# Transposing attention probabilities in row halves, and one written TensorE order for the dilated attention stage

## The chip, the cores and the metric

The kernel runs on one core of a Trainium2 chip. The metric is the device time of one execution in microseconds (us). Five queues of instructions matter here: TensorE (PE in the rows; its weight loads are shown apart as PEld), VectorE (DVE), ScalarE (ACT), GpSimd (POOL, idle here) and SyncE (SP), which issues the DMAs. Each runs its own list in order and waits on semaphores of the others.

## The reference, cut to what matters

The kernel is a two-layer encoder trunk over 256 tokens of width 1024. Layer 0 mixes tokens with a dilated attention (mixer A), layer 1 with a windowed grouped-query attention (mixer B). Each layer is FFN, mixer, FFN, gated embedding; the four FFNs are most of the work.

```python
for i in range(DEPTH):                                    # DEPTH = 2
    h = h + 0.5 * rms_norm(swiglu(rms_norm(h, g[0]), ffn_wi[i, 0], ffn_wo[i, 0]), g[1])
    hn = rms_norm(h, g[2])
    y = dilated_mixer(hn, ...) if i == 0 else window_gqa_mixer(hn, ...)
    h = h + rms_norm(y, g[3])
    h = h + 0.5 * rms_norm(swiglu(rms_norm(h, g[4]), ffn_wi[i, 1], ffn_wo[i, 1]), g[5])
    ...
# inside a mixer, per head: s = q @ k.T * dh**-0.5, masked; pr = exp(s - max); den = sum(pr)
#                           o = (pr @ v) / den;  then all heads: o @ wo
# mixer A: 3 dilation groups x 8 heads, outputs mixed by their denominators (one softmax over
#          the 512 allowed keys of the three groups); mixer B: 16 query heads on 4 key heads
```

## The kernel before, in words

The 256 tokens are two tiles of 128 (t = 0, 1). Weights are split into two float32r parts, so a projection of one tile against 512 columns is 24 multiplies (`proj`, L193; `rowprods`, L204). ScalarE makes the high part (L87) and VectorE the low part (L90) of every weight, all through the kernel.

**Mixer A** (`mixer_a`) runs nine projection blocks of 2 x 24 multiplies: values, queries and keys of three dilation groups. `block` leaves the transposition of queries and keys (`heads_T`, L316) pending, and the middle of the next block issues it. Then come eight *units*, each one token tile and one pair of heads: tile 0 with pairs 0 to 3, then tile 1. A unit n has these steps, which the rest of this document calls by letters:

- **S(n)**, `scores`: the logits of two heads (L325), 64 rows of the array for each head, one head on rows 0 to 63 and one on rows 64 to 127, into two PSUM banks "y" (four exist).
- the softmax (`soft`), for each of the two heads: on VectorE mask and maximum (L396), on ScalarE exponential with its sum (L397), on VectorE reciprocal (L398) and scaling (L399).
- **T(n)**, `transpose_p`: the scaled probabilities, four blocks of 128 x 128 for each head, by TensorE against the identity (L336) into one PSUM bank "t" for each head (two exist), copied to SBUF by ScalarE (L338).
- **PV(n)**, `values`: times the values (L414), one head on array columns 0 to 63, one on 64 to 127, into a bank "a"; ScalarE and VectorE split the result (L72, L73).

After four units `finish` multiplies tile 0 by the output weights (24 multiplies, L204) and `boundary` normalises and adds; the same for tile 1 at the end. `attend` emits these steps with S two units ahead of PV, but TensorE's list is set by the scheduler of the tile framework: only what stands inside one `tc.manual_schedule` (S of one unit, PV of one unit) keeps its written order there, and the scheduler weaves the pieces of several units into each other. The last projection block holds S(0) in its middle.

**Mixer B** has the same steps: its lines are L531 for S, L543, L546, L548 and L550 for the softmax (two halves of 256 keys for each head), the same `transpose_p` and L568 for PV, the same `attend`, and 48 multiplies for each output projection.

A multiply with plain float32 operands (all PV, all scores of mixer A) stands twice in the trace, once for each of its two passes; a transposition stands once.

Of the kernel before, what the change touches and what calls it, by code (L numbers as in the profile page):

```python
# [8 lines left out]
F32 = mybir.dt.float32  # L9
# [5 lines left out]
P = 128  # L15
# [4 lines left out]
DH = 64  # L20
# [17 lines left out]
def trunk_kernel(ctx, tc, x, p, norm_g, ffn_wi, ffn_wo, ple_proj, ple_gate, a_wqkv, a_wo,  # L38
                 b_wqkv, b_wo, b_sink, rope, mask_a, mask_b, out):
    nc = tc.nc  # L40
# [4 lines left out]
    wts = pool("wts", 9)  # L45
    hgs = pool("hgs", 1)
    m4 = pool("m4", M4)
    w2 = pool("w2", 12)
    ps_y = pool("ps_y", 4, space=bass.MemoryType.PSUM)
    ps_a = pool("ps_a", 2, space=bass.MemoryType.PSUM)  # L50
    ps_t = pool("ps_t", 2, space=bass.MemoryType.PSUM)
# [9 lines left out]
    def w2_tile(shape, dt=F32):  # L61
        return w2.tile(shape, dt, name="w2t", tag="w2t")
# [4 lines left out]
    def bank(which, shape=(P, 512)):  # L67
        pl = {"y": ps_y, "a": ps_a, "t": ps_t}[which]
        return pl.tile(list(shape), F32, name=f"ps{which}", tag=f"ps{which}")
# [260 lines left out]
    def pv_out(o_ps, oT, slot):  # L330
        split(oT[:, 0, slot, :], oT[:, 1, slot, :], o_ps[:, 0:P])

    def transpose_p(sm_of, kts):
        pt = bank("t")
        for i, a in enumerate(kts):
            nc.tensor.transpose(pt[:, i * P:(i + 1) * P], sm_of(a), ident)  # L336
        pT = w2_tile([P, 4, P])
        nc.scalar.copy(pT, pt.rearrange("p (n q) -> p n q", n=4))  # L338
        return pT

    def out_proj(t, oTs, ws, y):
# [2 lines left out]
    def mixer_a(acts, gb, row):  # L344
# [18 lines left out]
        def block(kind, g):  # L363
            ws = [weight_kt2(a_wqkv[0], c, ((kind * 3 + g) * 512,)) for c in range(4)]
            if kind == 2:
                dst = V[g] = m4_tile([P, 2, 512])
            else:
                dst = (qT, kT)[kind][g] = ([m4_tile([P, 4, 256], F32R) for _ in range(2)] if g == 0 and SPLIT_A
                                           else [m4_tile([P, 4, 256])])

            def one(t, mid=flush):
                ps = bank("a")
                proj(ps, acts[t], ws, mid)
                if kind == 2:
                    nc.scalar.activation(dst[:, t, :], ps, AF.Copy, scale=acts[t].rstd)  # L375
                    return
                q = w2_tile([P, 512])
                nc.scalar.activation(q, ps, AF.Copy, scale=nscale(t) if kind == 0 else acts[t].rstd)
                rope_(q, t, 8)
                pend.append(lambda: heads_T(q, dst, t, 4))  # L380
            return one
# [20 lines left out]
        oT, pTs = {}, {}  # L402

        def trans(t, pr):
            pTs[t, pr] = [transpose_p(lambda i: sm[:, i * P:(i + 1) * P], range(4)) for sm in sms.pop((t, pr))]

        def values(t, pr):
            pT = pTs.pop((t, pr))
            o_ps = bank("a")
            with tc.manual_schedule(engines={E.PE}):  # L410
                for i, (g, kt) in enumerate(((0, 0), (0, 1), (1, t), (2, t))):
                    for u in range(2):
                        hd = 2 * pr + u
                        nc.tensor.matmul(o_ps[64 * u:64 * u + 64, 0:P], V[g][:, kt, hd * DH:(hd + 1) * DH],  # L414
                                         pT[u][:, i, :], start=(i == 0), stop=(i == 3))
            if pr == 0:
                oT[t] = m4_tile([P, 2, 4, P], F32R)
            pv_out(o_ps, oT[t], pr)

        b0 = block(2, 0)  # L420
        b0(0)
        b1 = block(2, 1)
        b1(0, acts[1].fin)
        b0(1)
        b1(1)
        for g in range(3):
            for kind in range(2):
                b = block(kind, g)
                b(0)
                b(1)  # L430
        b = block(2, 2)
        b(0)
        sms = {}
        units = [(t, pr) for t in range(2) for pr in range(4)]

        def score(n):
            if n < len(units):
                sms[units[n]] = scores(*units[n])

        b(1, lambda: score(0))  # L440
        return attend(units, score, trans, values, 1,
                      [lambda k=k: weight_rows(a_wo[0], k) for k in range(4)],
                      lambda t: [oT[t]], gb, row)

    def attend(units, score, trans, values, done, wload, oTs, gb, row, flush=nothing):
        ahead = AHEAD
# [25 lines left out]
    def mixer_b(acts, gb, row):  # L472
# [80 lines left out]
        oT, pTs = {}, {}  # L553

        def trans(t, pr):
            pTs[t, pr] = [transpose_p(lambda n: sm[:, n // 2, (n % 2) * P:(n % 2 + 1) * P], range(4))
                          for sm in sms.pop((t, pr))]

        def values(t, pr):
            a, ih = pr // 2, pr % 2  # L560
            pT = pTs.pop((t, pr))
            o_ps = bank("a")
            with tc.manual_schedule(engines={E.PE}):
                for i in range(2):
                    for kt in range(2):
                        for u in range(2):
                            kv = 2 * a + u
                            nc.tensor.matmul(o_ps[64 * u:64 * u + 64, i * P:(i + 1) * P],  # L568
                                             V[:, kt, kv * DH:(kv + 1) * DH], pT[u][:, 2 * i + kt, :],
                                             start=(kt == 0), stop=(kt == 1))  # L570
            if ih == 0:
                oT[t, a] = m4_tile([P, 2, 4, P], F32R)
            o = oT[t, a]
            split(o[:, 0, 2 * ih:2 * ih + 2, :].rearrange("p n q -> p (n q)"),
                  o[:, 1, 2 * ih:2 * ih + 2, :].rearrange("p n q -> p (n q)"), o_ps[:, 0:256])
# [196 lines left out]
```

## Time and profile before

| | us |
|---|---|
| median of 3 runs (1093.93 to 1094.2) | 1093.97 |
| the profiled execution | 1094.63 |
| its span, first to last instruction | 1092.9 |
| TensorE busy | 1066.1 (98%) |
| VectorE busy | 694.8 (64%) |
| ScalarE busy | 570.6 (52%) |

Times in rows are microseconds from the start of the span. A matmul's busy time contains its latency in the pipeline, so that in a run of them the step from one start to the next start tells what they cost, and a TensorE that is 100% busy need not be at its peak. "PEclk" is the granted clock, 1.00 for 2.4 GHz and 0.50 for 1.2 GHz. What an engine waited for stands behind a row as [idle before <- releaser].

### The profile page before, as it was taken

The page shows a single profiled execution, that of the slowest core. Times are in us where ns is not written, and L with a number is a line of the kernel's source. Part 1 is how long each engine was busy: PE and PEld are TensorE (multiplying, and loading weights), DVE is VectorE, ACT ScalarE, POOL GpSimd, SP SyncE. Part 2 cuts the span into 40 slices and gives each one's busy share as a digit, 9 for nine tenths or more (in the row PEclk, how much of TensorE's full clock was granted, in tenths as well). Part 3 has the DMA queues.
Part 4 walks back from the last instruction along what each step waited for, and adds up shares of the span by engine and source line. Part 5 has one row for each costly group of instructions (what it writes and reads, how often), then busy time and mean ns, then how long its engine had stood idle before and what let it go on. Part 6 is the DMA issues. An engine that isn't in the chain of part 4 may idle for free.

```text
span 1092.9 us, 14763 instructions
## 1 busy us (share of the span) xinstructions
PE 1066.1 (98%) x5110; PEld 862.5 (79%) x5110; DVE 694.8 (64%) x1523; ACT 570.6 (52%) x896; POOL 0.7 (0%) x6
## 2 busy tenths in 40 slices
PE   7999999999999999999999999999998999999996
PEld 6888888788877888888887888887866888888885
DVE  6765454865666855576588654655975875557465
ACT  5644343655565645454456444544675665446343
POOL 0000000000000000000000000000000000000000
PEclk8999999999999999999999999999999999999998
DMA  8865655565540575576544756655660565567601
GB/s 268 294 199 176 204 182 165 174 221 164 174 135 30 165 229 187 161 246 205 163 138 154 233 170 195 193 162 167 178 170 1 158 214 180 171 211 241 202 1 39
DMA packets 130235, 189.04 MB, mean 173 GB/s; under 512 B 9440, under 2 KB 100320, under 8 KB 130160
## 3 DMA queue, kind: packets, MB, share of 16 engines
q1 hardware_dynamic: 130160, 188.10, 54.8%
q8 instruction: 40, 0.66, 0.2%
q14 instruction: 35, 0.29, 0.1%
HBM read 187.02 MB, written 1.05 MB: 172 GB/s over the span
## 4 chain that ended last, share of the span: by engine, by line
PE 93%; DVE 3%; ACT 2%; DMA 1%; issue 1%; SPq 1%; DVEq 0%; ACTq 0%
PE psa L193 54%; PE psy L204 29%; PE pst L240 2%; PE pst L336 2%; PE psa L414 1%; PE psa L630 1%; PE psy L325 1%; PE pst L146 1%; PE psa L568 1%; PE pst L316 1%; DMA raw<-in_ffn_wi_dram 1%; ACT w L87 1%; DVE w L90 1%; PE psa L187 1%; ACT w2t L338 0%
## 5 line engine op out<-in xcount | busy, mean ns | idle before, releaser
L193 PE MATMUL psa<-w,hgT 128*128 128x512 f32 x2664 | 632.7, 393 | 0.5 <-ACT m4t L375 0.5
L193 PEld LDWEIGHTS psa<-w,hgT 128*128 128x128 f32 x2664 | 494.9, 188 | 103.3 <-ACT m4t L375 0.9
L90 DVE TENSOR_TENSOR w<-raw,w 128x512 fp32r<-128x512 f32 x672 | 435.7, 687 | 174.6 <-ACT w L87 165.1
L87 ACT CAST w<-raw 128x1024 fp32r<-128x1024 f32 (+1 forms) x340 | 352.7, 1042 | 196.2 <-issue 82.3
L204 PE MATMUL psy<-w,w2t 128*128 128x512 f32 x1056 | 260.7, 399 | 2.6 <-ACT w2t L72 2.5
L204 PEld LDWEIGHTS psy<-w,w2t 128*128 128x128 f32 x1056 | 194.4, 188 | 47.8 <-ACT w2t L72 5.4
L231 ACT ACTIVATE w2t<-psa,small 128x256 f32<-128x256 f32 x88 | 41.7, 474 | 158.8 <-PE psa L193 154.5
L232 DVE SCALAR_TENSOR_TENSOR w2t<-psa,small,w2t 128x256 f32<-128x256 f32 x88 | 42.3, 481 | 115.0 <-ACT w2t L231 115.0
L73 DVE TENSOR_TENSOR w2t<-pst,w2t 128x256 fp32r<-128x256 f32 x88 | 36.5, 415 | 9.3 <-ACT w2t L72 9.3
L72 ACT CAST w2t<-pst 128x256 fp32r<-128x256 f32 x88 | 32.1, 364 | 10.1 <-PE pst L240 10.0
L204 PE MATMUL psy<-w,m4t 128*128 128x512 f32 x144 | 37.3, 402 | 0.0
L72 ACT CAST hgT<-w2t 128x512 fp32r<-128x512 f32 x32 | 19.4, 620 | 32.2 <-DVE w2t L148 32.0
L240 PE MATMUL pst<-ident,w2t 128*128 128x128 f32 x176 | 33.5, 271 | 1.5 <-DVE w2t L232 1.5
L240 PEld LDWEIGHTS pst<-ident,w2t 128*128 128x128 f32 x176 | 24.4, 139 | 13.2 <-issue 1.8
L204 PEld LDWEIGHTS psy<-w,m4t 128*128 128x128 f32 x144 | 25.9, 188 | 6.3 <-issue 1.2
L148 DVE TENSOR_TENSOR w2t<-pst,gcol 128x512 f32<-128x512 f32 x32 | 21.2, 685 | 10.9 <-PE pst L146 10.7
L336 PE MATMUL pst<-ident,w2t 128*128 128x128 f32 x128 | 21.4, 292 | 4.4 <-DVE w2t L550 4.3
L204 PE MATMUL psy<-w,hgT 128*128 128x512 f32 x96 | 23.4, 392 | 0.0
L336 PEld LDWEIGHTS pst<-ident,w2t 128*128 128x128 f32 x128 | 14.2, 144 | 11.3 <-issue 8.2
L114 ACT ACTIVATE w2t<-psy 128x512 f32<-128x512 f32 x24 | 14.2, 593 | 16.7 <-DVE w2t L166 16.6
L171 DVE SCALAR_TENSOR_TENSOR h<-w2t,small,h 128x512 f32<-128x512 f32 x32 | 22.6, 748 | 0.4
L204 PE MATMUL psy<-m4t,hgT 128*128 128x512 f32 x96 | 22.6, 389 | 0.0
(88 smaller groups left out, 551.7 us busy)
## 6 DMA issues: line engine op xcount, KB each, us to landing
raw<-in_ffn_wi_dram SPq DMA_DIRECT2D x352, 256.0 KB, 4.1
raw<-in_ffn_wo_dram SPq DMA_DIRECT2D x88, 512.0 KB, 4.9
raw<-in_a_wqkv_dram SPq DMA_DIRECT2D x36, 512.0 KB, 4.6
raw<-in_ple_gate_dram SPq DMA_DIRECT2D x16, 512.0 KB, 3.8
raw<-in_b_wqkv_dram SPq DMA_DIRECT2D x12, 512.0 KB, 4.0
gb<-in_norm_g_dram SPq DMA_DIRECT2D x8, 512.0 KB, 4.9
raw<-in_b_wo_dram SPq DMA_DIRECT2D x16, 256.0 KB, 5.7
raw<-in_a_wo_dram SPq DMA_DIRECT2D x4, 512.0 KB, 4.7
```

What stands on the lines that cost most here:

```text
L72: nc.scalar.copy(dst_hi, src)
L73: nc.vector.tensor_tensor(dst_lo, src, dst_hi.bitcast(F32), ALU.subtract)
L87: nc.scalar.copy(w[0][:, i:i + step], raw[:, i:i + step])
L90: nc.vector.tensor_tensor(w[1][:, c], raw[:, c], w[0][:, c].bitcast(F32), ALU.subtract)
L148: nc.vector.tensor_tensor(hg, pt.rearrange("p (k q) -> p k q", k=4), gcol[:, 4 * q:4 * q + 4, self.row].unsqueeze(2).broadcast_to([P, 4, P ...
L171: nc.vector.scalar_tensor_tensor(h[t][:, s], yg[i], r, h[t][:, s], ALU.mult, ALU.add)
L193: nc.tensor.matmul(ps, lhs(a, xh, 2 * c + k), ws[c][wh][:, k * 512:(k + 1) * 512], start=(c == 0 and k == 0 and n == 0), stop=(c == 3 and ...
L204: nc.tensor.matmul(y[half], lhsf(k, xh), ws[k][wh][:, half * 512:(half + 1) * 512], start=(first and k == 0 and i == 0), stop=(last and k ...
L231: nc.scalar.activation(su[:, 0, :], ps[:, 0:256], AF.Silu, scale=acts[t].rstd)
L232: nc.vector.scalar_tensor_tensor(su[:, 1, :], ps[:, 256:512], acts[t].rstd, su[:, 0, :], ALU.mult, ALU.mult)
L240: nc.tensor.transpose(pt[:, f * P:(f + 1) * P], su[:, 1, f * P:(f + 1) * P], ident)
L336: nc.tensor.transpose(pt[:, i * P:(i + 1) * P], sm_of(a), ident)
```

## The change

Three things change.

1. `transpose_p` takes both heads of a unit at once. Each 128 x 128 transposition becomes two, one for rows 0 to 63 and one for rows 64 to 127, issued in turn, each against a 64 x 64 piece of the identity. The upper halves go to one bank "t" and the lower halves to the other, so that a unit has 16 transpositions with 64 moving columns instead of 8 with 128. The two copies now copy one half of the rows for both heads, into one tile from a pool of its own (`pTp`, two buffers), and the pool `w2` goes from 12 to 10 buffers. Both mixers use it.
2. Mixer A computes the projections in another order: the values of groups 1 and 2 come last, and S(0), S(1) and S(2) stand between their halves, T(0) behind them (`lead`).
3. Mixer A no longer calls `attend` but `attend_in_order`, which writes TensorE's whole order from the lead to PV(7) inside one `manual_schedule`: T(n+1), S(n+3), PV(n). The output projection of tile 0 stands ahead of T(6).

```diff
-    w2 = pool("w2", 12)
+    w2 = pool("w2", 10)
+    pTp = pool("pTp", 2)
...
-    def transpose_p(sm_of, kts):
-        pt = bank("t")
-        for i, a in enumerate(kts):
-            nc.tensor.transpose(pt[:, i * P:(i + 1) * P], sm_of(a), ident)
-        pT = w2_tile([P, 4, P])
-        nc.scalar.copy(pT, pt.rearrange("p (n q) -> p n q", n=4))
+    def transpose_p(sms):
+        pts = [bank("t") for _ in range(2)]
+        with tc.manual_schedule(engines={E.PE}):
+            for n in range(8):
+                for hf in range(2):
+                    rows = slice(64 * hf, 64 * hf + 64)
+                    nc.tensor.transpose(pts[hf][:, n * 64:n * 64 + 64], sms[n // 4](n % 4)[rows, :], ident[rows, rows])
+        pT = pTp.tile([P, 2, 8, 64], F32, name="pT", tag="pT")
+        for hf in range(2):
+            nc.scalar.copy(pT[:, hf], pts[hf].rearrange("p (n q) -> p n q", n=8))
         return pT
...
-        b1 = block(2, 1)
+        b1 = block(0, 0)
...
-        for g in range(3):
-            for kind in range(2):
-                b = block(kind, g)
-                b(0)
-                b(1)
-        b = block(2, 2)
-        b(0)
+        for kind, g in ((1, 0), (0, 1), (1, 1), (0, 2), (1, 2)):
+            b = block(kind, g)
+            b(0)
+            b(1)
...
-        b(1, lambda: score(0))
-        return attend(units, score, trans, values, 1,
+        b1, b2 = block(2, 1), block(2, 2)
+
+        def lead():
+            b1(0)
+            score(0)
+            b1(1)
+            score(1)
+            b2(0)
+            score(2)
+            b2(1)
+            trans(*units[0])
+
+        return attend_in_order(units, score, trans, values, lead,
...
+    def attend_in_order(units, score, trans, values, lead, wload, oTs, gb, row):
...
+        with tc.manual_schedule(engines={E.PE}):
+            lead()
+            for n, u in enumerate(units):
+                if n == 5:
+                    finish(0)
+                if n + 1 < len(units):
+                    trans(*units[n + 1])
+                score(n + 3)
+                values(*u)
+        res[0].fin()
+        finish(1)
+        return res
```

How this moves instructions, at three places. TensorE in mixer A, about one unit of the steady part before (L325 scores, L336 transpositions, L414 values):

```order
L336 MATMUL pst<-ident,w2t 128x128 x4
L414 MATMUL psa<-w2t,m4t 64x128 x7
L325 MATMUL psy<-m4t 128x128 x3
L336 MATMUL pst<-ident,w2t 128x128 x4
L325 MATMUL psy<-m4t 128x128
L325 MATMUL psy<-m4t 128x256
L414 MATMUL psa<-w2t,m4t 64x128
```

The same engine after, from the last projection half on (L194 projections, L326 scores, L340 transpositions, L419 values):

```order
L194 MATMUL psa<-w,hgT_1862 128x512 x24
L340 MATMUL pst<-ident,w2t 128x64 x32
L326 MATMUL psy<-m4t 128x256 x2
L326 MATMUL psy<-m4t 128x128 x4
L419 MATMUL psa<-pT,m4t 64x128 x8
L340 MATMUL pst<-ident,w2t 128x64 x16
```

The steps of a unit are no longer cut into each other: T, S and PV each stand in one piece, and the transpositions stand right ahead of the scores.

ScalarE where the units of mixer A begin, before (L375 value projections, L87 weights, L397 exponentials, L338 copies of T, L72 split of PV):

```order
L375 ACTIVATE m4t<-psa,small 128x512
L87 CAST w<-raw 128x1024
L397 ACTIVATE w2t,small<-w2t,small 128x512
L87 CAST w<-raw 128x1024
L397 ACTIVATE w2t,small<-w2t,small 128x512
L338 COPY w2t<-pst 128x512 x2
L397 ACTIVATE w2t,small<-w2t,small 128x512
L72 CAST m4t<-psa 128x128
```

And after (L380, L88, L402, L343 and L73 are the same five):

```order
L380 ACTIVATE m4t<-psa,small 128x512
L88 CAST w<-raw 128x1024
L343 COPY pT<-pst 128x512 x4
L402 ACTIVATE w2t,small<-w2t,small 128x512
L73 CAST m4t<-psa 128x128
L343 COPY pT<-pst 128x512
L402 ACTIVATE w2t,small<-w2t,small 128x512
```

Six exponentials now stand ahead of these rows, in the lead; the four copies of T(0) and T(1) follow each other behind one value projection and one weight.

ScalarE in mixer B, one unit of the steady part before (L546 exponentials, L338 copies, L72 split of PV):

```order
L546 ACTIVATE w2t,pair<-w2t,pair 128x257
L338 COPY w2t<-pst 128x512
L546 ACTIVATE w2t,pair<-w2t,pair 128x257 x2
L338 COPY w2t<-pst 128x512
L546 ACTIVATE w2t,pair<-w2t,pair 128x257
L72 CAST m4t<-psa 128x256
```

And after (L582, L343 and L73 are the same three):

```order
L582 ACTIVATE w2t,pair<-w2t,pair 128x257
L343 COPY pT<-pst 128x512
L582 ACTIVATE w2t,pair<-w2t,pair 128x257
L343 COPY pT<-pst 128x512
L582 ACTIVATE w2t,pair<-w2t,pair 128x257 x2
L73 CAST m4t<-psa 128x256
```

A copy stood between the two exponentials of each head before; now the two copies of a unit stand around the second exponential of the next unit's first head. TensorE, VectorE and ScalarE have the same lists as before outside the two mixers, and SyncE and GpSimd everywhere.

## Rows read from the trace of the kernel before

**Rows 1.** The page: the chain that ended last, by engine.

```profile
PE 93%; DVE 3%; ACT 2%; DMA 1%; issue 1%; SPq 1%; DVEq 0%; ACTq 0%
```

**Rows 2.** Busy us by stretch: PE, PEld, DVE, ACT, POOL, then PEclk, DMA share, GB/s.

```profile
318.20:336.35 18.15, 18.15 (x159) 12.63 (x158) 11.72 (x41) 11.34 (x30) 0.00 (x0) 1.00 0.09 30
814.00:817.50 3.50, 3.28 (x19) 2.54 (x19) 1.96 (x11) 1.42 (x5) 0.00 (x0) 0.51 0.46 150
817.50:827.70 10.20, 7.25 (x64) 4.93 (x64) 5.77 (x29) 6.90 (x21) 0.00 (x0) 1.00 0.00 0
```

**Rows 3.** Timeline, TensorE in mixer A's units: start, busy, line, shape, count.

```profile
318.20 0.66 PE L336 MATMUL pst<-ident,w2t 128*128 128x128 f32 x4
318.79 1.09 PE L414 MATMUL psa<-w2t,m4t 128*64 128x128 f32 x14
...
321.66 0.43 PE L414 MATMUL psa<-w2t,m4t 128*64 128x128 f32 x2
...
335.33 1.09 PE L414 MATMUL psa<-w2t,m4t 128*64 128x128 f32 x14
```

**Rows 4.** Timeline, TensorE in mixer A: steps that stand in one piece, and the end.

```profile
312.12 1.15 PE L325 MATMUL psy<-m4t 64*128 64x256 f32 x12
...
337.52 5.03 PE L204 MATMUL psy<-w,m4t 128*128 128x512 f32 x21
342.48 1.15 PE L325 MATMUL psy<-m4t 64*128 64x256 f32 x12
343.56 1.09 PE L336 MATMUL pst<-ident,w2t 128*128 128x128 f32 x8
344.58 1.09 PE L414 MATMUL psa<-w2t,m4t 128*64 128x128 f32 x16
...
356.75 5.60 PE L193 MATMUL psa<-w,hgT 128*128 128x512 f32 x24
```

**Rows 5.** Timeline, weight loads of eight transpositions with 16 rows and 16 columns.

```profile
5.35 0.57 PEld L699 LDWEIGHTS pst<-ident,m4t 16*128 16x128 f32 x8
```

**Rows 6.** Timeline, ScalarE and VectorE in mixer A.

```profile
312.81 1.04 ACT L87 CAST w<-raw 128x1024 fp32r<-128x1024 f32 x1
...
320.79 1.06 ACT L338 COPY w2t<-pst 128x512 f32<-128x512 f32 x2
...
321.00 0.67 DVE L396 CUSTOM_DVE_ANT_0 w2t<-psy,msk 128x512 f32<-128x512 f32 x1
...
321.60 0.48 DVE L399 TENSOR_SCALAR w2t<-w2t,small 128x512 f32<-128x512 f32 x1
...
322.60 0.17 DVE L398 RECIPROCAL small<-small 128x1 f32<-128x1 f32 x1 [0.51 <-ACT w2t L397]
...
324.24 0.17 DVE L398 RECIPROCAL small<-small 128x1 f32<-128x1 f32 x1 [0.48 <-ACT w2t L397]
```

**Rows 7.** Timeline, mixer B: four of its sixteen reciprocals, a copy, an exponential.

```profile
804.43 0.17 DVE L548 RECIPROCAL pair<-pair 128x2 f32<-128x2 f32 x1 [0.65 <-ACT w2t L546]
...
822.40 0.17 DVE L548 RECIPROCAL pair<-pair 128x2 f32<-128x2 f32 x1 [1.16 <-ACT w2t L546]
...
824.08 0.58 ACT L338 COPY w2t<-pst 128x512 f32<-128x512 f32 x1 [0.16 <-PE pst L336]
824.56 0.51 ACT L546 ACTIVATE w2t<-w2t,pair 128x257 f32<-128x257 f32 x1
...
825.20 0.17 DVE L548 RECIPROCAL pair<-pair 128x2 f32<-128x2 f32 x1 [0.97 <-ACT w2t L546]
...
831.51 0.17 DVE L548 RECIPROCAL pair<-pair 128x2 f32<-128x2 f32 x1 [1.33 <-ACT w2t L546]
```

**Rows 8.** Timeline, mixer B with the output projection running: two more reciprocals.

```profile
839.43 0.17 DVE L548 RECIPROCAL pair<-pair 128x2 f32<-128x2 f32 x1 [0.67 <-ACT w2t L546]
...
841.59 0.17 DVE L548 RECIPROCAL pair<-pair 128x2 f32<-128x2 f32 x1 [0.67 <-ACT w2t L546]
```

**Rows 9.** The page's groups: the squares of a boundary (count, busy, mean ns of one, idle).

```profile
L114 ACT ACTIVATE w2t<-psy 128x512 f32<-128x512 f32 x24 | 14.2, 593 | 16.7 <-DVE w2t L166 16.6
```

More of the change, by code (lines that the diff above doesn't have):

```diff
@@ L404, in trans @@
         def trans(t, pr):
-            pTs[t, pr] = [transpose_p(lambda i: sm[:, i * P:(i + 1) * P], range(4)) for sm in sms.pop((t, pr))]
+            pTs[t, pr] = transpose_p([lambda i, sm=sm: sm[:, i * P:(i + 1) * P] for sm in sms.pop((t, pr))])
         def values(t, pr):
@@ L414, in values @@
                         nc.tensor.matmul(o_ps[64 * u:64 * u + 64, 0:P], V[g][:, kt, hd * DH:(hd + 1) * DH],
-                                         pT[u][:, i, :], start=(i == 0), stop=(i == 3))
+                                         pT[:, :, 4 * u + i, :], start=(i == 0), stop=(i == 3))
             if pr == 0:
@@ L438, in score, with finish @@
                 sms[units[n]] = scores(*units[n])
-        b(1, lambda: score(0))
-        return attend(units, score, trans, values, 1,
+        b1, b2 = block(2, 1), block(2, 2)
[9 more added lines that the diff above has]
+        return attend_in_order(units, score, trans, values, lead,
                       [lambda k=k: weight_rows(a_wo[0], k) for k in range(4)],
                       lambda t: [oT[t]], gb, row)
+    def attend_in_order(units, score, trans, values, lead, wload, oTs, gb, row):
+        res, ws = [], []
+        def finish(t):
+            if not ws:
+                ws.extend(f() for f in wload)
+            y = [bank("y") for _ in range(2)]
+            out_proj(t, oTs(t), ws, y)
+            res.append(boundary(t, y, gb, 1.0, row))
+        with tc.manual_schedule(engines={E.PE}):
[10 more added lines that the diff above has]
+        return res
     def attend(units, score, trans, values, done, wload, oTs, gb, row, flush=nothing):
@@ L555, in trans @@
         def trans(t, pr):
-            pTs[t, pr] = [transpose_p(lambda n: sm[:, n // 2, (n % 2) * P:(n % 2 + 1) * P], range(4))
-                          for sm in sms.pop((t, pr))]
+            pTs[t, pr] = transpose_p([lambda n, sm=sm: sm[:, n // 2, (n % 2) * P:(n % 2 + 1) * P]
+                                      for sm in sms.pop((t, pr))])
         def values(t, pr):
@@ L568, in values @@
                             nc.tensor.matmul(o_ps[64 * u:64 * u + 64, i * P:(i + 1) * P],
-                                             V[:, kt, kv * DH:(kv + 1) * DH], pT[u][:, 2 * i + kt, :],
+                                             V[:, kt, kv * DH:(kv + 1) * DH], pT[:, :, 4 * u + 2 * i + kt, :],
                                              start=(kt == 0), stop=(kt == 1))
```

## Prediction, made before the changed kernel was run

> **What bounds the kernel now.** I read the page first: on the chain of work that ended last TensorE holds 93% of the span [rows 1], so an edit pays where it shortens TensorE's list or a wait in it. The busy times by stretch then tell the two mixers apart. In mixer A, from 318.20 to 336.35, TensorE is busy without a gap while VectorE and ScalarE are busy for 11.72 and 11.34 of 18.15 us [rows 2]: A is bound by TensorE's own list. The timeline shows what that list pays for. From one PV to the same piece of the fourth PV after it, 318.79 to 335.33, a unit takes 16.54 / 4 = 4.13 us [rows 3]. Standing in one piece, S takes 1.08 (342.48 to 343.56), T takes 1.02 (343.56 to 344.58) and PV is busy for 1.09 [rows 4], some 3.1 together. The difference is cutting: four transpositions on their own take 0.59 where eight take 1.02 [rows 3, 4], so each costs 0.108 and each change of array shape a fixed 0.16; and two instructions of PV split from their partners on the other array half are busy for 0.43, where sixteen in pairs need 1.09 [rows 3, 4]. Mixer B is another matter. Its softmax moves in halves of one head each, 2.80 us from reciprocal to reciprocal (822.40 to 825.20) [rows 7]; VectorE and ScalarE answer each other there, and the copy of T stands in the middle of that chain (copy at 824.08, next exponential at 824.56 as soon as it ends). TensorE waits for them.
>
> **The cost of T in halves.** The trace has no transposition of 64 rows. Bounds: eight weight loads of 128 columns for transpositions with 16 moving columns took 0.57 us in all [rows 5], about 0.062 apart once the last one's own 0.13 is taken off. If the upper and the lower half run side by side, a unit has eight such steps, 0.5 us; if one after the other, sixteen, 1.0 us; today it is 8 x 0.108 = 0.87. The nearest row for the first case is S: its two heads stand on the same two row halves, in two banks, and its twelve instructions are busy for 1.15 us in all [rows 4], while PV's sixteen fit into 1.09 only as pairs. I take 0.5 for a unit, and keep 1.0 as the other end.
>
> The trace shows those loads 0.062 apart. The Trainium skill (TensorE: Matmul & The Clock Gate, section LDWEIGHTS (loading the stationary operand)) gives columns / 1.2 ns whatever the rows, so 107 ns for 128 columns; by that rule an estimated 8 x 0.107 = 0.86 for a unit, and T would gain nothing. The row for transpositions says 62 ns, so the measurement decides, but the rule's result is in my first rival.
>
> **Mixer A, step by step.** What moves at no cost: the nine projection blocks keep their count of multiplies and of pending transpositions, and their weights come in the order in which they are used; TensorE covers that supply as now. The smaller pool `w2` holds at most six softmax tiles in the lead, of ten. If that cover fails, a wait of one unit's length appears in the lead.
>
> - *Lead.* At 312.12 TensorE has done all projections and S(0) [rows 4]. The change puts S(1) and S(2) ahead of that point too, each 1.08 and about 0.2 more for the second change of shape: T(0) starts at 312.12 + 2.6 = 314.7.
> - *A new wait.* T(1) stands right behind T(0) and needs both banks "t", so both copies of T(0). ScalarE has the result of a value projection (no row here; I put 0.6, a little over one copy of T) and a weight (1.04) ahead of the copies, which take 1.06 for two [rows 6]. T(1) starts some 2.8 after T(0), at 317.5, and TensorE waits for over 2 us. Queued behind it are S(3) and PV(0). T(1) and S(3) are done at 319.1.
> - *Steady part.* TensorE needs S 0.9, T 0.5, PV 0.87 and two changes of 0.16, 2.6 us a unit, so it is no longer the bound. VectorE's list is now mask, reciprocal, mask, scale, reciprocal, scale. The second softmax takes 1.64, from one reciprocal to the next (322.60 to 324.24); then come the scaling (0.48 busy, 0.4 as a step), the next mask (0.67) and its exponential, 1.60 from the mask at 321.00 to the reciprocal at 322.60 [rows 6]: 0.1 + 0.4 + 1.6 = 2.1. A unit takes 1.64 + 2.1 = 3.7 us, not 4.13.
> - *To the output projection.* T(5) needs the softmax of unit 5: two periods and 3.9 us for its own two heads, 319.1 + 7.4 + 3.9 = 330.4. S(7) and PV(4) take 2.2, so the projection of tile 0 starts at 332.7, and its 24 multiplies end at 338.3 (21 were busy for 5.03 [rows 4]).
> - *End.* T(6) and PV(5) take 1.6, to 339.9. The copies of T(6) stand behind the two squares of the boundary on ScalarE, 0.59 each [rows 9], and those behind VectorE's two products: they end near 341.2, and T(7) waits for that. T(7), its copies, PV(6) and PV(7) reach 344.0, eight transpositions of the new activations 344.9, and the remaining 22 multiplies 350.0. Today the next FFN starts at 356.75 [rows 4].
>
> That is 6.7 us. I take 6.0, since the first FFN weights of ScalarE now come behind the transposed activations and can hold TensorE for a part of a microsecond. Ends: 4.0 if halves cost 1.0 each (T(0), T(1), T(6) and T(7) are on the path, the others lie under VectorE's chain), 7.5 if ScalarE takes its weight after the copies.
>
> **Mixer B.** It keeps `attend` and the scheduler. T in halves needs both heads' softmax before either copy can start, and ScalarE now has both copies around one exponential. So one half of a unit still has T and a copy in its chain, 2.80 [rows 7], about 0.1 more since ten scores stand ahead of it and it is itself 0.1 shorter; the other half has none. The trace shows such a half where T is out of the chain: 839.43 to 841.59, 2.16 [rows 8]. A unit takes 2.80 + 0.1 + 2.16 = 5.1 instead of 5.6. Over four and a half units (nine halves lie between 804.43 and 831.51 [rows 7]) that gives 2.3 us. Against it, three groups of transpositions stand among the output projection's multiplies, where a change of array shape is new: about 0.3 each, and the pair of groups behind S saves 0.4. Sum for B: 2.3 - 0.9 + 0.4, about 2.0. Ends: -1 and 4.
>
> **Sum.** 6.0 + 2.0 = 8.0. The profiled execution, 1094.63 us, becomes 1086.6; it lay 0.66 above the median of 1093.97, so on the scale of the median the forecast is 1086.0.
>
> **Rivals.**
> - *Halves cost as much as wholes*, by a slow load or because they don't run side by side; the change then doesn't do in T what it says. For it: no row shows two transpositions at once. Against it: S does it with the same rows and banks. A keeps 4.0, for its order is repaired all the same; B gets 2.3 less 0.3 for the longer T in each of its five chains, less some 1.2 in the projections: -0.4. Together 3.6: 1090.4.
> - *B loses to the clock.* The granted clock fell to 0.51 from 814.00 to 817.50, after TensorE had waited in every half, and stood at 1.00 for the ten us after that [rows 2]. The nine halves took 27.08 instead of 25.2 [rows 7], so the half clock costs B 1.9 today. Shorter transpositions leave TensorE with less work between its waits; if every second half were stretched by 0.6, B would lose 4 x 0.6 against today's 1.9, and with the changes of shape its gain falls to zero or a little under: total 5.5, 1088.5.
> - *Slower: A at half clock.* A now makes TensorE wait: over 2 us at T(1), then 1.1 of every 3.7. If the clock fell to 1.2 GHz there and stayed, S, T and PV double, 2.3 to 4.6, and a unit takes some 5.2. From T(0) to PV(7) eight units lose 1.5 each against 3.7, 12 us; A ends 6 slower than now, and the total 4 to 6 slower: 1098 to 1100. It decides from about two thirds of that stretch at 0.5 (8 us lost eats the whole gain). Against it: B waits more than that today (7.25 us busy of 10.20) and held 1.00 there [rows 2].
>
> **How the numbers follow.** Forecast 1086.0, chance 0.66, with its own range 1083.5 to 1088. Halves as costly as wholes: 0.16. B loses to the clock: 0.11, inside the range. Slower: 0.05. Other small things that leave it within 0.2%, 0.02. The range must leave out at most 2 in 10: from 1083.5 to 1090.5 it holds the forecast's own, the second rival and most of the first. A measurement of this kernel tells about 0.2%, 2.2 us, from no change: faster is below 1091.8. Faster 0.89, same 0.06, slower 0.05.
>
> **What would show it.** In the profile after: T as sixteen instructions that are busy for some 0.7 us (right) or over 1.1 (first rival); units of A 3.7 apart, ended by waits for the softmax and no longer by TensorE; a wait of over 2 us ahead of T(1); the FFN behind A starting about 6 us earlier; reciprocals of B alternating near 2.2 and 2.9; PEclk 1.00 through A. The prediction is wrong if T(1) waits much longer, if A's units stay over 4, or if B's halves all stay at 2.8.

## The result, and the profile after

The changed kernel takes 1087.36 us (median of 4 runs, 1086.1 to 1087.86), beside 1094.09 for the kernel before in the same session (4 runs, 1093.93 to 1094.69): a ratio of 0.9936, with a 95% interval from 0.9924 to 0.9948. The forecast was 1086.0 with a range from 1083.5 to 1090.5. The sum was about right, and its parts were not: mixer A gave a little more than forecast, mixer B nothing.

The table cuts each profiled execution where a projection starts, from the start of the first multiply of one stage to that of the next (the start times come from the trace; mixer A goes from its first projection to the FFN behind it).

| stage | before, us | after, us |
|---|---|---|
| start to mixer A | 205.34 | 205.56 |
| mixer A | 151.40 | 145.05 |
| FFNs and embedding between the mixers | 410.60 | 409.98 |
| mixer B | 98.13 | 98.10 |
| FFN and end | 227.38 | 227.38 |

The profiled executions, 1094.63 and 1087.86, differ by 6.77, of which A has 6.35. The 0.62 between the mixers is spread over 1844 multiplies, of which none has more than 0.03 of it, in code that is the same. The kernels of the next section lie between 409.9 and 410.3 there, and the part ahead of mixer A, the same in all, between 204.6 and 206.9; so I count a few tenths as spread between executions.

TensorE's timeline of the changed kernel in mixer A (start, busy time, line, shape, count, and in brackets the idle time before and its releaser; L340 is T, L326 S, L419 PV, L205 the output projection, L194 the FFN behind) answers to [rows 3, 4]:

```profile
314.91 0.71 PE L340 MATMUL pst<-ident,w2t 64*128 64x64 f32 x16
317.17 0.27 PE L340 MATMUL pst<-ident,w2t 64*128 64x64 f32 x1 [1.56 <-ACT pT L343]
317.66 0.71 PE L340 MATMUL pst<-ident,w2t 64*128 64x64 f32 x15 [0.22 <-ACT pT L343]
318.15 1.15 PE L326 MATMUL psy<-m4t 64*128 64x256 f32 x12
319.23 1.09 PE L419 MATMUL psa<-pT,m4t 128*64 128x128 f32 x16
...
325.98 0.24 PE L340 MATMUL pst<-ident,w2t 64*128 64x64 f32 x1 [0.32 <-DVE w2t L404]
326.81 0.71 PE L340 MATMUL pst<-ident,w2t 64*128 64x64 f32 x15 [0.58 <-ACT pT L343]
327.36 1.09 PE L326 MATMUL psy<-m4t 64*128 64x256 f32 x12
329.80 0.24 PE L340 MATMUL pst<-ident,w2t 64*128 64x64 f32 x1 [0.32 <-DVE w2t L404]
...
333.22 5.74 PE L205 MATMUL psy<-w,m4t 128*128 128x512 f32 x24
338.89 0.71 PE L340 MATMUL pst<-ident,w2t 64*128 64x64 f32 x16
...
350.61 1.75 PE L194 MATMUL psa<-w,hgT 128*128 128x512 f32 x7
```

S, T and PV stand in one piece each. Sixteen half transpositions are busy for 0.71 us, where eight whole ones took 1.09 [rows 4]. From T to T a unit takes 3.82 us (325.98 to 329.80), and these two T wait for VectorE's scaling (L404) and then for ScalarE's copy (L343): TensorE is no longer the bound there. (The two units ahead of them take 2.60 and 2.74 from PV to PV, with no wait of their T in the rows.) The FFN behind starts at 350.61, not at 356.75 [rows 4]. VectorE's reciprocals in the same stretch, 1.64 and 2.17 apart, answer to [rows 6]:

```profile
324.68 0.17 DVE L403 RECIPROCAL small<-small 128x1 f32<-128x1 f32 x1 [0.88 <-ACT w2t L402]
...
326.32 0.16 DVE L403 RECIPROCAL small<-small 128x1 f32<-128x1 f32 x1 [0.28 <-ACT w2t L402]
...
328.49 0.16 DVE L403 RECIPROCAL small<-small 128x1 f32<-128x1 f32 x1 [0.88 <-ACT w2t L402]
```

Mixer B: the reciprocals of the changed kernel, one for each half of a unit, answer to [rows 7]; under them the stretches that matter (PE, PEld, DVE, ACT, POOL busy, then PEclk, DMA share, GB/s), which answer to [rows 2].

```profile
816.77 0.17 DVE L584 RECIPROCAL pair<-pair 128x2 f32<-128x2 f32 x1 [1.96 <-ACT w2t L582]
818.92 0.17 DVE L584 RECIPROCAL pair<-pair 128x2 f32<-128x2 f32 x1 [0.67 <-ACT w2t L582]
822.58 0.17 DVE L584 RECIPROCAL pair<-pair 128x2 f32<-128x2 f32 x1 [1.84 <-ACT w2t L582]
824.73 0.17 DVE L584 RECIPROCAL pair<-pair 128x2 f32<-128x2 f32 x1 [0.67 <-ACT w2t L582]
827.48 0.17 DVE L584 RECIPROCAL pair<-pair 128x2 f32<-128x2 f32 x1 [0.92 <-ACT w2t L582]
```

```profile
797.62:824.73 27.11, 21.58 (x201) 17.11 (x199) 19.03 (x87) 18.10 (x51) 0.00 (x0) 0.69 0.19 59
...
801.40:815.05 13.65, 12.21 (x90) 9.63 (x89) 10.46 (x42) 7.92 (x25) 0.00 (x0) 0.50 0.25 78
...
818.50:821.90 3.40, 3.19 (x30) 2.56 (x26) 1.82 (x8) 1.70 (x6) 0.00 (x0) 0.50 0.00 0
821.90:826.00 4.10, 2.92 (x40) 2.30 (x41) 2.75 (x13) 3.30 (x11) 0.00 (x0) 1.00 0.00 0
```

The halves alternate as forecast, but the long one has two prices. Where TensorE has 2.4 GHz it is 2.75 (824.73 to 827.48), and a unit is 2.75 + 2.15 = 4.90. Where a part of it falls into a stretch at 1.2 GHz it is 3.66 (818.92 to 822.58). The changed kernel spends 17.1 us of B at 1.2 GHz (13.65 and 3.41 long), the kernel before 6.8 (two of 3.41), and the same nine halves take 27.11 after and 27.08 before.

The waits of TensorE in that part of B, of the kernel before (first fence, L336 and L568 are T and PV) and of the changed one (second; L604 is PV, L340 T, L317 a transposition of queries); columns are the total, the count and the longest:

```profile
PE pst L336 <- DVE w2t L550: 3.9, 6, 1.0
PE psa L568 <- ACT w2t L338: 1.4, 4, 0.5
```

```profile
PE psa L604 <- ACT pT L343: 4.2, 3, 1.6
PE pst L340 <- ACT w L88: 1.0, 1, 1.0
PE pst L317 <- ACT pT L343: 0.2, 1, 0.2
```

Before, TensorE waited ten times for at most 1.0 us. After, PV needs both copies of a unit, of which the second stands behind an exponential, and TensorE stands still in fewer and longer pieces of up to 1.6. The two counts are not quite alike, for 17.1 us of the second stretch run at 1.2 GHz, where TensorE's own work takes longer and fills a part of what would be a wait. What came ahead of the first fall of the clock is much the same in both (first row the kernel before, second the changed one): TensorE was busy for 2.10 of 3.40 us and for 2.38 of 3.50. What differs is how long the clock then stayed down, 3.41 and 13.65 us.

```profile
810.60:814.00 3.40, 2.10 (x19) 1.35 (x17) 3.40 (x14) 2.22 (x7) 0.00 (x0) 1.00 0.48 148
797.90:801.40 3.50, 2.38 (x34) 1.85 (x31) 3.50 (x23) 3.50 (x9) 0.00 (x0) 1.00 0.48 154
```

### The profile page after: what moved, and what is told of

Its sections match the earlier page's. It is cut to its first block, busy times and chain, and to the rows that moved or that the text cites. A ratio compares the mean times of both kernels' runs of the same rounds, so it can differ in the third digit from the quotient of the medians.

```text
span 1086.1 us, 15021 instructions
## 1 busy us (share of the span) xinstructions
PE 1057.2 (97%) x5238; PEld 860.5 (79%) x5238; DVE 694.2 (64%) x1523; ACT 570.7 (53%) x896; POOL 0.7 (0%) x6
## 4 chain that ended last, share of the span: by engine, by line
PE 92%; ACT 3%; DVE 3%; issue 1%; DMA 1%; SPq 1%; DVEq 0%; ACTq 0%
PE psa L194 54%; PE psy L205 29%; PE pst L241 2%; PE psa L604 1%; PE psa L666 1%; PE pst L147 1%; PE pst L340 1%; PE pst L317 1%; ACT w L88 1%; ACT pT L343 1%; DMA raw<-in_ffn_wi_dram 1%; PE psa L188 1%; ACT w2t L402 1%; PE psy L567 1%; DVE w2t L401 0%
## 5 line engine op out<-in xcount | busy, mean ns | idle before, releaser
L194 PE MATMUL psa<-w,hgT 128*128 128x512 f32 x2664 | 633.1, 393 | 0.5 <-ACT m4t L380 0.5
L194 PEld LDWEIGHTS psa<-w,hgT 128*128 128x128 f32 x2664 | 494.7, 188 | 103.1 <-ACT m4t L380 0.9
L88 ACT CAST w<-raw 128x1024 fp32r<-128x1024 f32 (+1 forms) x340 | 352.8, 1042 | 191.4 <-issue 87.0
L205 PE MATMUL psy<-w,w2t 128*128 128x512 f32 x1056 | 260.1, 398 | 2.5 <-ACT w2t L73 2.5
L205 PEld LDWEIGHTS psy<-w,w2t 128*128 128x128 f32 x1056 | 194.4, 188 | 47.3 <-ACT w2t L73 5.4
L73 ACT CAST w2t<-pst 128x256 fp32r<-128x256 f32 x88 | 32.1, 365 | 10.2 <-PE pst L241 9.9
L73 ACT CAST hgT<-w2t 128x512 fp32r<-128x512 f32 x32 | 19.5, 620 | 33.8 <-DVE w2t L149 33.6
L205 PE MATMUL psy<-w,m4t 128*128 128x512 f32 x144 | 35.9, 399 | 0.0
L241 PE MATMUL pst<-ident,w2t 128*128 128x128 f32 x176 | 33.5, 271 | 1.5 <-DVE w2t L233 1.5
L241 PEld LDWEIGHTS pst<-ident,w2t 128*128 128x128 f32 x176 | 24.5, 140 | 13.1 <-issue 1.8
L205 PEld LDWEIGHTS psy<-w,m4t 128*128 128x128 f32 x144 | 26.2, 188 | 6.1 <-DVE small L401 0.2
L205 PE MATMUL psy<-w,hgT 128*128 128x512 f32 x96 | 23.4, 392 | 0.0
L205 PE MATMUL psy<-m4t,hgT 128*128 128x512 f32 x96 | 22.6, 389 | 0.0
L74 DVE TENSOR_TENSOR hgT<-w2t,hgT 128x512 fp32r<-128x512 f32 x32 | 21.4, 687 | 0.8 <-ACT hgT L73 0.4
L205 PEld LDWEIGHTS psy<-m4t,hgT 128*128 128x128 f32 x96 | 18.0, 188 | 3.8
```

The lines of the kernel that those rows point to most:

```text
L73: nc.scalar.copy(dst_hi, src)
L74: nc.vector.tensor_tensor(dst_lo, src, dst_hi.bitcast(F32), ALU.subtract)
L88: nc.scalar.copy(w[0][:, i:i + step], raw[:, i:i + step])
L194: nc.tensor.matmul(ps, lhs(a, xh, 2 * c + k), ws[c][wh][:, k * 512:(k + 1) * 512], start=(c == 0 and k == 0 and n == 0), stop=(c == 3 and ...
L205: nc.tensor.matmul(y[half], lhsf(k, xh), ws[k][wh][:, half * 512:(half + 1) * 512], start=(first and k == 0 and i == 0), stop=(last and k ...
L241: nc.tensor.transpose(pt[:, f * P:(f + 1) * P], su[:, 1, f * P:(f + 1) * P], ident)
```

## The experiments

All numbers of stages are from one profiled execution of each kernel, cut as in the table above. "Nine halves" goes from the first to the tenth reciprocal of B. The kernel before took 1093.66 in the sessions of e1 to e8 and 1094.38 in that of e9 and e10, 1094.09 beside the changed kernel, so tenths between the times of different rows mean nothing, and a ratio is to the kernel before in the same session.

| kernel | A | B | nine halves, PEclk over them | B at 1.2 GHz | time |
|---|---|---|---|---|---|
| before | 151.40 | 98.13 | 27.08, 0.87 | 6.8 | 1094.09 |
| changed | 145.05 | 98.10 | 27.11, 0.69 | 17.1 | 1087.36 |
| e1: new order, whole T | 144.68 | 97.27 | 26.25, 0.93 | 3.4 | 1086.37, one run |
| e1t: the same, timed | 144.69 | 97.74 | 26.68, 0.87 | 6.8 | 1086.64 |
| e2: old order, halves | 149.78 | 100.27 | 27.00, 0.64 | 23.9 | 1094.15, one run |
| e4: one half after the other | 144.83 | 106.87 | 29.70, 0.56 | 34.1 | 1096.05, one run |
| e5: T(0) earlier | 144.21 | 100.18 | 26.88, 0.64 | 23.9 | 1090.25 |
| e6: fillers in all of B | 145.06 | 96.10 | 22.11, 1.00 | 0 | 1087.72, one run |
| e7: fillers in five units | 146.43 | 93.04 | 22.11, 1.00 | 0 | 1084.24 |
| e8: as e7, whole T in B | 145.10 | 95.53 | 24.55, 1.00 | 0 | 1086.31, one run |
| e9: as e7, whole T in A | 144.70 | 93.12 | 22.11, 1.00 | 0 | 1082.95 |
| e10: as e9, T(0) earlier | 143.76 | 93.06 | 22.11, 1.00 | 0 | 1081.40 |

**The order alone.** Mixer A keeps its new written order, and both mixers transpose whole blocks again, each head into one bank with its copy behind it. (The index of the copied tile in PV changes with it; it is not printed here.)

```diff
-    def transpose_p(sms):
+    def transpose_p(sms, whole=False):
+        if whole:
+            pT = pTp.tile([P, 2, 8, 64], F32, name="pT", tag="pT")
+            for u, sm_of in enumerate(sms):
+                pt = bank("t")
+                for i in range(4):
+                    nc.tensor.transpose(pt[:, i * P:(i + 1) * P], sm_of(i), ident)
+                nc.scalar.copy(pT[:, u], pt.rearrange("p (n q) -> p n q", n=8))
+            return pT
```

> The written order of mixer A with the old whole transpositions (eight of 128 rows for a unit, one copy for each head) in both mixers. Theory (in A the order carries most of the gain, since VectorE's and ScalarE's chain sets the pace there; halves count only for T(0), T(1), T(6) and T(7), about 0.37 us each): mixer A takes 146.5 us against 145.05 in the changed kernel and 151.4 before, units still 3.8 apart, total 1088.9. Rival (the halves carry it): A 149 or more, units over 4.0 apart, total over 1091.

> The new order of mixer A with P transposed whole in both mixers, the same edit as in the single look e1_order_only, now timed. Theory (the order carries the whole gain of A, the halves none of it, and in B whole transpositions leave TensorE less time at half clock): mixer A 144.5 to 144.9 us as in the single look, B 97 to 98, the time 1086.0 to 1087.0, that is 0.3 to 1.0 us below the changed kernel. Rival (the single look was a lucky run, and the halves are worth what the prediction gave them, about 0.4 us of each unit of A): A above 146, the time 1088.5 or more.

A takes 144.68 and 144.69, the whole gain and 0.37 more than with halves, where the first run was expected to take 146.5; the ratio of e1t to before is 0.9936 (0.9920 to 0.9951) against 0.9936 for the whole change. So the halves add nothing to the total that these runs can tell, and A's gain is the order's. TensorE of the timed one (T(0), T(1), S(3), then the output projection of tile 0 and the FFN behind):

```profile
315.56 1.03 PE L340 MATMUL pst<-ident,w2t 128*128 128x128 f32 x8
316.97 1.15 PE L340 MATMUL pst<-ident,w2t 128*128 128x128 f32 x8 [0.38 <-ACT pT L341]
318.05 1.15 PE L326 MATMUL psy<-m4t 64*128 64x256 f32 x12
...
334.10 5.74 PE L205 MATMUL psy<-w,m4t 128*128 128x512 f32 x24
...
350.97 1.75 PE L194 MATMUL psa<-w,hgT 128*128 128x512 f32 x7
```

Whole transpositions do cost time in the units: from S(3) to the output projection 16.05 us pass here (318.05 to 334.10) and 15.07 in the changed kernel (318.15 to 333.22). What the halves save there is spent on either side of it: from T(0) to S(3) 2.49 us pass here and 3.24 in the changed kernel, from the output projection to the FFN 16.87 and 17.39. ScalarE's rows show why at T(1), first of the changed kernel (L88 a weight, L343 the copies of T(0)), then of e1t (L341 the copies):

```profile
315.60 1.03 ACT L88 CAST w<-raw 128x1024 fp32r<-128x1024 f32 x1
316.53 1.07 ACT L343 COPY pT<-pst 128x512 f32<-128x512 f32 x2
```

```profile
316.34 1.06 ACT L341 COPY pT<-pst 128x512 f32<-128x512 f32 x2
317.29 1.06 ACT L88 CAST w<-raw 128x1024 fp32r<-128x1024 f32 x1
```

In the changed kernel T(0) is done at 315.62 (314.91 and 0.71), but ScalarE makes a weight first, and T(1) starts 2.26 us after T(0); in e1t the copies go ahead of the weight, and it is 1.41. The same stands at T(7): with halves both copies of T(6) lie behind the boundary's two squares on ScalarE, with whole blocks the first copy goes between them. The scheduler sets this order, no line of the edit does. The weight comes first wherever the halves alternate in A behind this lead (the changed kernel, e6, e7, e8), the copies where one bank is full before the other (e1, e1t, e4, e9); that this is the scheduler's reason is not shown. So e1 against the changed kernel compares two lists of ScalarE as well as two kinds of T.

**The halves alone.** The kernel before, with the new `transpose_p` and its pool; mixer A keeps the old order.

```diff
-        return attend_in_order(units, score, trans, values, lead,
+        return attend(units, score, trans, values, 1,
```

> The halves, the new pool and both copies as in the changed kernel, but mixer A with the old order of projections and the old loop, TensorE's list left to the scheduler. Theory: TensorE stays the bound in A, each unit is 0.4 shorter by T and saves a change of shape or two, but steps stay cut into each other: A 148 us, total 1090. Rival (the halves carry it): A 146 or less. Other rival (order alone matters): A 150.5 or more.

A gains 1.62 us in the old order, less than the 3.4 expected and more than the rival's 0.9 (3.4 us of A run at 1.2 GHz, so it might be some more), and B loses 2.14; the time is that of before, not the 1090 expected. The two gains of A don't add: 6.71 for the order, 1.62 for the halves, 6.35 together. In the written order, what a shorter T saves in the units goes into the waits for ScalarE around them.

**One half after the other.** The two loops of the transposition are exchanged, so that eight upper halves come first and then eight lower ones.

```diff
-            for n in range(8):
-                for hf in range(2):
+            for hf in range(2):
+                for n in range(8):
```

> The changed kernel with all eight upper transpositions of a unit ahead of its eight lower ones. Theory (neighbours in the list run side by side only where they are on different row halves): T takes 16 x 0.061 = 1.0 instead of 0.5 us, A 147 us (four of the eight T on the path), total 1089.5. Rival (two halves overlap whatever their order, or the weight load sets the pace alone): T stays at 0.5, A at 145.05, total 1087.4.

The first two transpositions of A on TensorE's timeline:

```profile
314.63 1.01 PE L340 MATMUL pst<-ident,w2t 64*128 64x64 f32 x16
316.02 1.01 PE L340 MATMUL pst<-ident,w2t 64*128 64x64 f32 x13 [0.37 <-ACT pT L343]
```

And the part of B at 1.2 GHz (PEclk is 1.00 through the units of A, 318.00 to 333.00):

```profile
800.80:834.90 34.10, 30.36 (x202) 23.16 (x201) 19.82 (x85) 18.05 (x55) 0.00 (x0) 0.50 0.10 32
```

T takes 1.01 instead of 0.71 busy: the gain of the halves is that upper and lower run side by side, and needs the alternation. The Trainium skill (TensorEngine Tiling (Array Packing), section Key Properties) says that different tiles of the array can load weights and multiply in parallel; 0.71 with alternation against 1.01 without agrees. A is not slower for it (144.83, where 147 was expected), for ScalarE's copies of T(0) stand ahead of the weight again and T(1) starts 1.39 after T(0): T can be twice as long in A at no cost. B loses 8.8 us to the changed kernel, which neither expectation had, and TensorE runs at 1.2 GHz for all of 800.80 to 834.90. What share of the 8.8 is the clock's and what the longer T's was not tried apart.

**Fillers in B.** Four multiplies of the identity by itself stand ahead of each PV, into the bank that PV then overwrites. They do no work that anything reads. First in all units of B (e6, `range(4)`), then in the first five only (e7, shown here).

```diff
             with tc.manual_schedule(engines={E.PE}):
+                for _ in range(4 if t == 0 or pr == 0 else 0):
+                    nc.tensor.matmul(o_ps[:, 0:P], ident, ident, start=True, stop=True)
                 for i in range(2):
```

> The changed kernel with four extra multiplies of the identity by itself (128 x 128, float32, 0.21 us each) ahead of PV in every unit of mixer B, written into the bank that PV then overwrites: work that TensorE does while it would wait. Theory (in B the gain went to the half clock, which TensorE's short work between waits brings on): granted clock 1.00 through B, halves of the softmax alternate 2.15 and 2.75, B 98.1 less 5 plus about 1 for extra changes of shape at the end, 94 to 95 us, total 1084. Rival (the two copies around one exponential or the changes of shape ate the gain): B 98.5 to 100 whatever the clock, total 1088 to 1089.

> The changed kernel with four multiplies more ahead of PV in the first five units of mixer B, whose results PV overwrites; units 5 to 7, where TensorE has the out projection to do, have none. Theory (the halves are worth about 0.75 us a unit in B at full clock, and the changed kernel lost all of it to 17 us at half clock; in e6_b_fill4 the fillers of the last three units took back about 3 us, since nothing waits there): TensorE at full clock through B, the nine reciprocals of units 0 to 4 in 22.1 us as in e6 instead of 27.1, and B in 93.0 to 94.0 us instead of 98.1; the time 1082.5 to 1083.7. Rival (B's end is set by the loads of its out projection's weights or by another chain, and the earlier units only wait longer there): B 96 to 97, the time 1085.5 to 1086.5.

The clock stays at 2.4 GHz through B, and nine halves take 22.11 in both, five us less than in the changed kernel, from the same chain of softmax, T and copy (e7's reciprocals, and then its stretches):

```profile
814.84 0.17 DVE L584 RECIPROCAL pair<-pair 128x2 f32<-128x2 f32 x1 [0.92 <-ACT w2t L582]
816.99 0.17 DVE L584 RECIPROCAL pair<-pair 128x2 f32<-128x2 f32 x1 [0.67 <-ACT w2t L582]
819.74 0.17 DVE L584 RECIPROCAL pair<-pair 128x2 f32<-128x2 f32 x1 [0.92 <-ACT w2t L582]
```

```profile
799.78:821.89 22.11, 21.39 (x241) 17.34 (x239) 18.73 (x87) 18.30 (x51) 0.00 (x0) 1.00 0.25 74
318.30:321.70 3.40, 3.23 (x31) 3.01 (x33) 0.84 (x2) 1.19 (x3) 0.00 (x0) 0.50 1.01 351
```

From the third unit on each is 2.15 + 2.75, the price that the changed kernel's own trace shows where its clock is full. The fillers also move some steps in the lists of ScalarE and VectorE, around the copies of T(0); from 812.59 on the changed kernel's lists of these two are those of e7. So of the five us, the 2.3 of the two long halves behind that time (4.18 and 3.66 instead of 2.75) go with the clock, and the 2.7 ahead of it may in part be the lists'. The cleanest price is the changed kernel's own: 3.66 and 2.75 for the same steps at either clock. In e6 the fillers of the last three units stand in TensorE's list where it has the output projection to do, and cost 3.06 us of B (96.10 against 93.04), so that e6 missed the 94 to 95 expected of B and, at 1087.72, the 1084; without them B comes out as expected. The total, 1084.24 (ratio 0.9908, 0.9888 to 0.9927), is some 0.5 above what was expected: in e7's profiled execution the clock also fell for 3.4 us at T(1) of A, after the 2 us wait there (last row), and A took 1.4 more.

**Whole transpositions in B with the same fillers.** To e7, with the `whole` branch of e1 and its index in PV (not printed here):

```diff
-                                      for sm in sms.pop((t, pr))])
+                                      for sm in sms.pop((t, pr))], True)
```

> As e7_b_fill_first5, but with P transposed whole in mixer B (A as in the changed kernel). It says what the halves themselves are worth in B when neither kernel runs at half clock. Theory (halves 0.75 us a unit, over five units): no half clock in B, the nine reciprocals of units 0 to 4 in 25.5 to 26.3 us, units 2.8 us a reciprocal, B 96.3 to 97.3, some 3 us above e7. Rival (the halves are worth nothing, and all that e7 or e6 gain is the clock): nine reciprocals in 22.1 us and B equal to that of e7 within 0.5 us.

```profile
798.76:823.31 24.55, 24.19 (x218) 18.94 (x216) 19.23 (x88) 18.93 (x53) 0.00 (x0) 1.00 0.22 66
```

Neither expectation was met. Nine halves take 24.55 us, between the two, and B is 2.5 above e7. At full clock the halves are thus worth some 2.4 us in B, beside the fillers. This holds for that pair only: in e8 TensorE is busy for 24.19 of the 24.55 (the row above), so with whole transpositions the fillers themselves may be a part of its bound. No run had whole transpositions and a full clock without fillers. The halves of e1 outside its slow stretch, 2.80 and 2.85, would make a unit 5.65, 0.75 above 4.90.

**T(0) earlier.** In the lead T(0) goes ahead of the last value projection (the expectations call it a Q projection), so that its copies run under that projection.

```diff
             score(2)
+            trans(*units[0])
             b2(1)
-            trans(*units[0])
```

> The changed kernel with one step moved: T(0), the first transposition of A, stands ahead of the last Q projection of the lead instead of behind it, so that ScalarE can copy it out while TensorE projects. Theory (the 1.78 + 0.49 us wait ahead of T(1) is a wait for ScalarE's two copies, which stood behind a weight cast, and it lies on A's path): the wait goes to under 0.6 us, the first reciprocal of A's steady stretch comes 1.3 to 1.9 us earlier and mixer A takes 143.2 to 144.0 instead of 145.05; the time falls to 1085.3 to 1086.3. Rival (A's end is set by ScalarE and VectorE or by the weights, not by this wait): A 144.8 to 145.2, the time as of the changed kernel, 1087.4. Rival on the other side (the step ahead of the last projection waits for the softmax of the first unit): A 145.5 or more.

```profile
314.55 0.71 PE L340 MATMUL pst<-ident,w2t 64*128 64x64 f32 x16
```

On TensorE's timeline of e5 the wait is gone, and T(1) runs straight behind the projection. A gains 0.84, less than half of the wait; the later T still wait for the chain of softmax and copies. The total missed every expectation: 1090.25 (6 runs, 1085.94 to 1090.74), ratio 0.9961 (0.9944 to 0.9977), above the changed kernel's 0.9936, though the two intervals overlap at their ends. In the profiled execution, 1088.24, B has 23.9 us at 1.2 GHz and takes 2.08 more, which eats the gain in A. No trace was taken of the four runs from 1090.22 to 1090.74, so where their last 2 us lie is open; their mean granted clock over the whole execution, 0.985 and 0.986, is higher than the 0.981 of the profiled one, so it is not in more time at 1.2 GHz.

**The parts together.** To e7, in mixer A (with the `whole` branch of e1 and its index in PV, and for the second the two lines of e5 too):

```diff
-            pTs[t, pr] = transpose_p([lambda i, sm=sm: sm[:, i * P:(i + 1) * P] for sm in sms.pop((t, pr))])
+            pTs[t, pr] = transpose_p([lambda i, sm=sm: sm[:, i * P:(i + 1) * P] for sm in sms.pop((t, pr))], True)
```

> The parts that the runs so far found worth something, put together: the new order of mixer A with P transposed whole in A, halves in mixer B, and the four fillers ahead of PV in B's first five units. Theory (the order carries A's gain, the halves are worth some 2.5 us in B once TensorE keeps its clock): A 144.5 to 144.9 us as in e1_order_only, without the 1.78 us wait ahead of T(1) in which e7_b_fill_first5 showed 3.4 us at half clock in A, B 92.8 to 93.3 as in e7, the time 1081.5 to 1083.0. Rival (what is saved in A shifts B into stretches at half clock again, as in e5_t0_early): half clock in B, B above 95, the time 1084 or more.

> As e9_a_whole_b_fill, with T(0) of mixer A ahead of the lead's last Q projection, as in e5_t0_early. Theory (the wait ahead of T(1) is ScalarE's, and with whole transpositions 0.65 us of it was left): A 143.8 to 144.3 us, B as in e9, the time 0.4 to 0.9 us below e9. Rival (A's end is set from its out projections on, which wait for nothing that the step moves): A within 0.2 us of e9 and the same time.

With whole blocks in A, halves in B and fillers in B's first five units the kernel takes 1082.95, ratio 0.9893 (0.9879 to 0.9908), below both kernels. With T(0) earlier too it takes 1081.40, 0.9888 (0.9871 to 0.9904). The intervals of these two overlap; the traces show A 0.94 us shorter, about what e5 gained there, and B the same. With B's clock held the step's gain in A is no longer eaten in B; that the total keeps it is not shown beyond the overlap.

## Why the prediction was right, and where not

- **T in halves, 0.5 us a unit: right.** Sixteen busy for 0.71, beside "some 0.7" forecast, and fifteen take 0.55 from their start to that of S (326.81 to 327.36); side by side, as e4 shows. The Trainium skill's rule that the prediction names (TensorE: Matmul & The Clock Gate, section LDWEIGHTS (loading the stationary operand)) gave an estimated 0.86; the trace does not agree.
- **A's lead: right to a few tenths.** T(0) at 314.91 (314.7 forecast); T(1) after a wait of 1.56 + 0.22 us by the rows (over 2 us forecast), its fifteen from 317.66 on (317.5); S(3) done at 319.23 (319.1).
- **A's unit: 3.82 instead of 3.7.** The second softmax took 1.64 as forecast, the step behind it 2.17 instead of 2.1. Two periods make half of the 0.5 by which everything behind is late: the output projection at 333.22 (332.7), the FFN at 350.61 (350.0). A gave 6.35, between the 6.0 that I took and the 6.7 worked out.
- **What A owes to the halves: wrong.** The lower end of A's term, 4.0, and the first rival priced whole transpositions at half a microsecond for each of T(0), T(1), T(6) and T(7) "on the path". e1 shows 0.4 less A with them, not 2 us more. The step counted TensorE's time in T alone; around T(1) and T(7) the wait for ScalarE ends last, and its list came out another way with whole blocks, with the copies ahead of the weight and of the second square. That gives back more than the 0.98 that whole blocks cost in the units, which the prediction had put at nothing. If the halves had not run side by side, A would have lost nothing, as e4 shows (144.83).
- **B's term, 2.0: the step that failed.** Its own sum, 2.3 - 0.9 + 0.4, is 1.8. The mechanism was right: one half with T in its chain, one without, 2.75 + 2.15 where 5.1 was forecast. At full clock, with fillers, nine halves take 22.11, five less than before. But the term took the clock of before for granted, 6.8 us of B at 1.2 GHz, and the changed kernel has 17.1. The price that decided is the second rival's, TensorE at 1.2 GHz, which had 0.11. It forecast every second half longer by 0.6; the trace shows 3.66, 4.18 and 4.19 for the three long halves that meet a stretch at 1.2 GHz, instead of 2.75, and B's gain fell to 0.03. Its reason, that shorter transpositions leave TensorE with less work, is not borne out: in e4 T is as long as a whole one, and its stretch at 1.2 GHz is the longest. The total stayed in a range that was chosen to hold this rival, and by luck it lies nearer to the forecast than the parts do: A gave 0.35 more than I took, and 0.62 of the profiled difference lies in code that is the same.
- **The clock in A: as forecast here, with little to spare.** PEclk is 1.00 through the units, as the row below shows, so the slower case did not come; e7's execution shows that it can for one stretch of 3.4 us, at a cost of 1.4.

```profile
318.20:333.22 15.02, 13.21 (x209) 11.18 (x205) 9.46 (x33) 10.95 (x28) 0.00 (x0) 1.00 0.24 84
```

What stays open is what makes a slow stretch last. The kernels with whole transpositions and no fillers show 3.4 to 6.8 us of it in B, the four with halves and no fillers 17.1 to 34.1, and the change in the waits (ten of at most 1.0 us, then five of up to 1.6) is the difference in the rows that stands beside it. That more work on TensorE ends it shows that how TensorE's time is filled decides it; which of length and number of waits counts was not tried apart, and the length of T alone does not (e4). The lengths are also of one execution each: the changed kernel's mean granted clock is 0.985 in the profiled execution and 0.987 to 0.989 in the three others, which had less time at 1.2 GHz, and no trace shows where.

## What to carry to other kernels

Where an engine's list is cut up by a scheduler, write its order first: here that was the whole gain, and what the cheaper instruction saved on its engine went into waits for the next one, whose list was still the scheduler's. So look at what the consumer does ahead of the step's copies (here a weight of 1.03 us), not only at how long the step takes. An edit that changes how TensorE waits has to be priced at the clock that it will then get; a few multiplies of no use, only where TensorE would stand still, gained five us of mixer B here, the cheaper transposition, beside them, some 2.4.

## What the runs showed of the hardware that was not expected

Less time in transpositions went with more time at the lower clock: with halves that alternate, B ran 17.1 to 23.9 us at 1.2 GHz instead of 3.4 to 6.8, although no wait there was longer than 1.6 us in the changed kernel. The shorter work is not the cause by itself, for e4, whose T is as long as a whole one, ran 34.1. The Trainium skill (TensorE: Matmul & The Clock Gate, section A second HAM failure mode: psum-queue depth-cycling) tells of a kernel whose clock swung because TensorE idled briefly between groups of multiplies; these rows agree, and in e6 to e10 four more multiplies a unit kept the clock at 1.00 throughout B.

Half transpositions cost as much as whole ones if they come one half after the other: sixteen are busy for 1.01 us in e4, eight whole ones for 1.03 in e1t.
